# Modulation sums as products with a column of ones, and a third buffer for the modulation's weight rows

## The chip, the core and the metric

The kernel runs on one core of a Trainium2 chip. A core has five engines that work side by side, each in the order of its own queue: TensorE (PE in the profile, its weight loads PEld) multiplies, VectorE (DVE) and ScalarE (ACT) work element by element, GpSimd (POOL) does odd jobs, and SyncE (SP) issues the DMA transfers. SBUF is the working memory of 128 partitions; TensorE writes its results to PSUM, which is divided into banks. The metric is the time of one execution on the device in microseconds, as the median of several runs.

## What is computed

A decoder trunk of two layers on 256 tokens with 2048 channels, all in float32. In each layer six modulation vectors come from one condition vector `c`; they scale and shift the inputs of the two sub-layers and gate their outputs.

```python
cond = jax.nn.silu(c)
for l in range(DEPTH):
    mod = (jnp.einsum('bd,de->be', cond, w_ada[l]) + b_ada[l]).reshape(B, N_MOD, 1, D_MODEL)
    sh_m, sc_m, gt_m, sh_f, sc_f, gt_f = [mod[:, i] for i in range(N_MOD)]
    u = x * (1 + sc_m) + sh_m
    proj = u @ w_in[l]
    y_attn = sliding_window_attention(q, k, v, attn_sinks[l], cos, sin)
    y_rwkv, v_first = rwkv7_group(...)
    mix = jnp.concatenate([y_attn, y_rwkv], axis=-1) @ w_out[l]
    x = layer_norm(DEEPNORM_ALPHA * x + gt_m * mix, ln1_w[l], ln1_b[l])
    u = x * (1 + sc_f) + sh_f
    gate, up = jnp.split(u @ w_gate_up[l], 2, axis=-1)
    x = layer_norm(DEEPNORM_ALPHA * x + gt_f * ((jax.nn.silu(gate) * up) @ w_down[l]), ln2_w[l], ln2_b[l])
```

The modulation is a product of one vector of 2048 with a matrix of 2048 x 12288 in each layer, 201 MB of weights in all, each of which is used once.

## The kernel before

**The weight stream.** The large products (`w_in`, `w_out`, `w_gate_up`, `w_down`) read their weights tile by tile through `steps` (L364 on): a tile `raw` of 128 x 1024 comes in by DMA (L372, four buffers), ScalarE rounds it to `hi` (L380), VectorE takes the rest as `lo` (L381), and TensorE forms three products of 128 x 512 (L402, L403, L405) or, turned round, of 128 x 256 (L414 to L416).

**The modulation.** It isn't done by TensorE, as a product with one row would leave it nearly empty. A unit is half a modulation vector, 1024 columns (`ada_steps`). For each of 16 row blocks a tile `ast` of 128 x 1024 comes in (L253, 512 KB, two buffers), and VectorE adds `ast` times its piece of `cond`, one scalar for each partition, to the sum `aacc` (L255 for the first, L257 for the others). Then `ada_sums` adds up `aacc` over the partitions: each of the 8 blocks of 128 x 128 is transposed by TensorE into a PSUM bank (L277), ScalarE copies the transposed block onto itself with an accumulated sum over the row (L281, two instructions in the profile: the copy and the reading of the accumulator) into a column of `asum`, and VectorE adds the bias and stores the vector in `mods` (L284). There are 20 such units. The two first modulation vectors of layer 0 are needed before anything else and are made in the opening by `ada_first`, in five parts of 4, 4, 2, 4 and 2 column blocks with eight buffers of their own (L301, L306); each part calls `ada_sums` twice, and then `make_u` transposes the input (L354) and makes `u` of it (L358 to L361).

**Banks.** `bank()` gives out two PSUM banks in turn; in the opening one of the two is held for a projection, so that all calls of `bank()` share the other.

**Order.** The 20 units run beside the weight stream: the generator `ada_rest` is moved on by so many rows after each weight tile (`pump`), in the recurrence (`adv(AR)`), and after each step of the attention (`adv(AA)`). A note of dependence (`anchor`) places each L257 behind the last `lo` before it. Tile's planner simulates the whole program on a time line and from it gives each engine its fixed order; on the chip each engine then waits in that order. All transfers are issued by SP, in one order: a transfer whose buffer isn't free yet, or whose source isn't written, holds up what is behind it.

**The mixer and the attention.** A layer's mixer runs the recurrent group (decays, project, prepare, invert, recur, close) and the attention, in an order written out by hand (`ORDER`). `invert` sends small matrices through DRAM: nb from nscr (L727), a loop on GpSimd, tinv from ttl (L738), tm from tinv (L741). The attention has for each of four key heads `rotate` (a), `weigh` (b) and `gather` (c). `rotate` loads `qk` (L888, L889, one buffer), multiplies it by the cosines into `ra` (L894) and by the sines into `rb` (L895), and combines both to `qr` in four instructions (L898, L899). `gather` transposes the weights of four heads (L964 to L966), copies each from PSUM into a `pts` (L969 on ScalarE for odd heads, L971 on VectorE for even ones, three buffers) and multiplies with the values (L977 to L981), heads 0 and 1 first, then 2 and 3. The attention's pool takes the place of the pool that the recurrent group needs before.

Of the kernel before, what the change touches and what calls it, by code (L numbers as in the profile page):

```python
# [10 lines left out]
F32 = mybir.dt.float32  # L11
F32R = mybir.dt.float32r
I32 = mybir.dt.int32
AF = mybir.ActivationFunctionType
ALU = mybir.AluOpType
AX = mybir.AxisListType
# [3 lines left out]
P = 128  # L20
# [24 lines left out]
PARTS = (4, 4, 2, 4, 2)  # L45
LAG = 2
WB = (4, 3, 2)
RED = 1
AR = (3, 7)
AA = (1, 45)  # L50
AP = (0.65, 0.3)
# [16 lines left out]
def hybrid_trunk_kernel(  # L68
# [21 lines left out]
    def bank(name="mb", tag="mb"):  # L90

        if tag == "cb":
            return ps.tile([P, 512], F32, tag="cb", name=name)
        t = f"m{turn[0]}"
        turn[0] ^= turn[1]
        return ps.tile([P, 512], F32, tag=t, name=name, bufs=1)
# [149 lines left out]
    def ada_steps(l, mod, c0):  # L246

        src = w_ada[l].rearrange("(j p) n -> p j n", p=P)
        n0 = mod * D + c0
        acc = adap.tile([P, 1024], F32, tag="aacc", name="aacc")  # L250
        for j in range(KT):
            t = adap.tile([P, 1024], F32, tag="ast", name="ast", bufs=2)
            dma(t, src[:, j, n0:n0 + 1024])  # L253
            if j == 0:
                V.tensor_scalar_mul(acc, t, cond[:, 0:1])  # L255
            else:
                ins = V.scalar_tensor_tensor(acc, t, cond[:, j:j + 1], acc, ALU.mult, ALU.add)  # L257
                if anchor:
                    tc.add_manual_dep(ins.ins, anchor[0], order, reason="behind the weight stream")
            yield  # L260
        for _ in range(LAG):
            yield

        ada_sums(l, mod, c0, [acc[:, i * P:(i + 1) * P] for i in range(8)])
        done.add((l, mod, c0 // 1024))
        yield

    def ada_sums(l, mod, c0, blocks):

        col = mod * KT + c0 // P  # L270
        n = len(blocks)
        sm = adap.tile([P, 8], F32, tag="asum", name="asum", bufs=2)
        for q in range(0, n, 4):
            b = bank()
            m = min(4, n - q)
            for i in range(m):
                PE.transpose(b[:, i * P:(i + 1) * P], blocks[q + i], ident)  # L277
            for i in range(m):
                bi = b[:, i * P:(i + 1) * P]
                if RED:  # L280
                    S.activation(bi, bi, AF.Copy, accum_out=sm[:, q + i:q + i + 1])  # L281
            if not RED:
                V.reduce_sum(sm[:, q:q + m], b[:, 0:m * P].rearrange("p (i k) -> p i k", k=P), axis=AX.X)
        V.scalar_tensor_tensor(mods[l][:, col:col + n], sm[:, 0:n], 1.0 if mod in (1, 4) else 0.0,  # L284
                               prm(l, "b_ada", col, n), ALU.add, ALU.add)
        if mod in (2, 5):
            row = adap.tile([8, P], F32, tag="arow", name="arow", bufs=2)[0:n]
            rb = bank()
            PE.transpose(rb[0:n, 0:P], mods[l][:, col:col + n], ident)
            S.copy(row, rb[0:n, 0:P])  # L290
            dma(gates[l, mod // 3, c0 // P:c0 // P + n], row)
# [198 lines left out]
    def mixer(l, us, mixp, feeds):  # L490
# [33 lines left out]
        if l > 0:  # L524
# [3 lines left out]
            b = bank()  # L528
# [355 lines left out]
        def rotate(kv):  # L884
            qk = pt.tile([P, 2, 320], F32, tag="qk", name="qk", bufs=1)
            vt = pt.tile([P, 2, 64], F32, tag="vt", name="vt", bufs=4)
            qd = qkv[l].rearrange("t p n -> p t n")
            dma(qk[:, :, 0:256], qd[:, :, kv * 256:(kv + 1) * 256])  # L888
            dma(qk[:, :, 256:320], qd[:, :, AW + kv * 64:AW + (kv + 1) * 64])  # L889
            dma(vt, qd[:, :, AW + KVW + kv * 64:AW + KVW + (kv + 1) * 64])  # L890
            ra = pt.tile([P, 2, 10, 32], F32, tag="ra", name="ra", bufs=1)
            rb = pt.tile([P, 2, 10, 32], F32, tag="rb", name="rb", bufs=1)
            sv = qk.rearrange("p t (h d) -> p t h d", d=32)
            V.tensor_mul(ra, sv, cosk.unsqueeze(2).to_broadcast([P, 2, 10, 32]))  # L894
            V.tensor_mul(rb, sv, sink_.unsqueeze(2).to_broadcast([P, 2, 10, 32]))  # L895
            qr = pt.tile([P, 2, 6, 64], F32, tag="qr", name="qr", bufs=1)
            for t in range(2):
                V.tensor_sub(qr[:, t, 0:5, 0:32], ra[:, t, 0::2, :], rb[:, t, 1::2, :])  # L898
                V.tensor_add(qr[:, t, 0:5, 32:64], ra[:, t, 1::2, :], rb[:, t, 0::2, :])  # L899
            G.tensor_copy(qr[:, :, 5, :], qr[:, :, 4, :])  # L900
            qT = pt.tile([P, 3, T], F32, tag="qT", name="qT", bufs=2)
            for j0, nj in ((0, 2), (2, 1)):
                b = abank(0)
                for j in range(nj):
                    for t in range(2):
                        PE.transpose(b[:, j * T + t * P:j * T + (t + 1) * P],
                                     qr[:, t, 2 * (j0 + j):2 * (j0 + j) + 2, :].rearrange("p h d -> p (h d)"), ident)
                if j0 == 0:
                    S.copy(qT[:, 0:2, :].rearrange("p a t -> p (a t)"), b)
                else:  # L910
                    S.activation(qT[:, 2, :], b[:, 0:T], AF.Copy, scale=0.125)
            at[kv] = qT, vt
# [46 lines left out]
        def gather(kv):  # L959
            pp, vt = at[kv]  # L960
            pts = {}
            for h in range(4):
                b = abank(2)
                PE.transpose(b[:, 0:P], pp[1, h][:, 0:P], ident)  # L964
                PE.transpose(b[:, P:2 * P], pp[1, h][:, P:2 * P], ident)
                PE.transpose(b[:, 2 * P:3 * P], pp[0, h], ident)  # L966
                pts[h] = pt.tile([P, 3 * P], F32, tag="pts", name="pts", bufs=3)
                if h % 2:
                    S.copy(pts[h], b[:, 0:3 * P])  # L969
                else:  # L970
                    V.tensor_copy(pts[h], b[:, 0:3 * P])  # L971
            yb = abank(3)
            for h2 in range(0, 4, 2):
                o = (h2 // 2) * T
                two = [(h, slice(64 * (h % 2), 64 * (h % 2) + 64)) for h in (h2, h2 + 1)]
                for h, hs in two:
                    PE.matmul(yb[hs, o:o + P], lhsT=vt[:, 0, :], rhs=pts[h][:, 2 * P:3 * P], start=True, stop=True)  # L977
                for h, hs in two:
                    PE.matmul(yb[hs, o + P:o + 2 * P], lhsT=vt[:, 0, :], rhs=pts[h][:, 0:P], start=True, stop=False)
                for h, hs in two:  # L980
                    PE.matmul(yb[hs, o + P:o + 2 * P], lhsT=vt[:, 1, :], rhs=pts[h][:, P:2 * P], start=False, stop=True)  # L981
            for j in range(2):
                keep_y(2 * kv + j, yb[:, j * T:(j + 1) * T])
# [364 lines left out]
```

## Time and profile before

| | |
|---|---|
| median of 3 runs | 2715.88 us (2715.45 to 2717.28) |
| the profiled execution | 2716.41 us, its span 2714.6 us |
| first row tile of a unit issued | 56.4 us |
| last row tile of a unit issued | 1666.9 us |
| last modulation vector stored | 1754.3 us |
| row tiles of the 20 units, 512 KB each | 320 |
| blocks summed by L277, L281 | 192 |

The tables of the profile are read like this. A row of a stretch has its window, its length, and then for each engine the busy time with the count of instructions, the granted clock of TensorE, the busy share of the 16 DMA engines and their rate in GB/s. A row of a group has line, engine, operation, output and inputs, shape and count, then the busy time in us, the mean of one in ns, and the idle time of that engine just before, with what ended it. A row of the waits has who waited for whom: total in us, times, longest. A row in the order of time has the start and the length in us; instructions that follow one another with the same line are one row with their count; what stands in brackets is the engine's idle time ahead of it and what ended it. Matmul ends are modelled: a plain pass of 128 columns is shown with some 0.27 us, though the next may start 0.11 us after it.

### The profile page before, as it was taken

How to read it: one execution, taken by the hardware profiler on the slowest of the kernel's cores; microseconds unless marked ns; L12 is line 12 of the kernel's file. 1: busy time of each engine (PE TensorE's matmuls, PEld its weight loads, DVE VectorE, ACT ScalarE, POOL GpSimd, SP SyncE). 2: the span in 40 equal slices, each digit the busy share in tenths (PEclk: the TensorE clock that was granted, in tenths of full speed). 3: DMA queues.
4: the chain of work that ended last, by engine and by line, in shares of the span. 5: the costliest groups of instructions: out<-in, count | busy, mean ns of one | idle time of the engine just before them, and what ended most of it. 6: DMA issues, size and time to landing. Idle time of an engine off the chain costs nothing. (4 is left out here: it accounts for less than half of the span.)

```text
span 2714.6 us, 41774 instructions
## 1 busy us (share of the span) xinstructions
PE 2517.3 (93%) x15325; PEld 2103.9 (78%) x15325; DVE 1853.5 (68%) x2437; ACT 1188.4 (44%) x2029; POOL 180.0 (7%) x387
## 2 busy tenths in 40 slices
PE   3789998797999999999999989989899999999998
PEld 2787886575788888888889877867788888888887
DVE  6877767879777777777788677565764545545456
ACT  2364452434444444444445544534444444344442
POOL 1002111003000000000000022110120000000000
PEclk9799997798999999999999999979999999999999
DMA  9968667597888888889888586423746655566654
GB/s 310 382 193 254 203 197 225 179 331 250 313 318 308 303 307 304 294 302 309 304 287 288 175 251 204 116 75 130 258 163 190 190 190 190 194 191 189 190 190 148
DMA packets 351999, 637.49 MB, mean 235 GB/s; under 512 B 75894, under 2 KB 142898, under 8 KB 350258
## 3 DMA queue, kind: packets, MB, share of 16 engines
q1 hardware_dynamic: 351794, 634.82, 71.1%
q8 instruction: 120, 1.97, 0.3%
q14 instruction: 85, 0.70, 0.1%
HBM read 622.08 MB, written 12.62 MB: 234 GB/s over the span
## 5 line engine op out<-in xcount | busy, mean ns | idle before, releaser
L380 ACT CAST hi<-raw 128x1024 fp32r<-128x1024 f32 (+2 forms) x728 | 757.8, 1044 | 1097.6 <-PE acc L405 810.6
L381 DVE TENSOR_TENSOR lo<-raw,hi 128x1024 fp32r<-128x1024 f32 (+2 forms) x728 | 885.9, 1220 | 515.8 <-PE acc L403 335.2
L403 PE MATMUL acc<-lo,u 128*128 128x512 f32 x1568 | 515.7, 396 | 16.9 <-DVE lo L381 16.6
L405 PE MATMUL acc<-hi,u 128*128 128x512 f32 x1568 | 507.3, 392 | 0.0
L257 DVE SCALAR_TENSOR_TENSOR aacc<-ast,cond,aacc 128x1024 f32<-128x1024 f32 x300 | 388.7, 1296 | 136.2 <-DMA ast<-in_w_ada_dram 135.1
L402 PE MATMUL acc<-hi,u 128*128 128x512 f32 x1568 | 459.7, 395 | 2.4 <-ACT u L360 1.1
L403 PEld LDWEIGHTS acc<-lo,u 128*128 128x128 f32 x1568 | 294.6, 189 | 83.9 <-DVE lo L381 23.7
L402 PEld LDWEIGHTS acc<-hi,u 128*128 128x128 f32 x1568 | 295.8, 189 | 65.4 <-ACT u L360 1.8
L405 PEld LDWEIGHTS acc<-hi,u 128*128 128x128 f32 x1568 | 296.4, 189 | 62.3 <-issue 0.7
L403 PE MATMUL acc<-lo,ht 128*128 128x512 f32 (+1 forms) x720 | 243.7, 377 | 2.7 <-DVE lo L381 2.6
L405 PE MATMUL acc<-hi,ht 128*128 128x512 f32 (+1 forms) x720 | 242.3, 375 | 0.0
L414 PE MATMUL acc<-u,hi 128*128 128x256 f32 x720 | 206.4, 293 | 12.9 <-ACT hi L380 12.9
L402 PE MATMUL acc<-hi,ht 128*128 128x512 f32 (+1 forms) x720 | 217.1, 376 | 0.0
L415 PE MATMUL acc<-u,hi 128*128 128x256 f32 x720 | 205.6, 292 | 0.0
L416 PE MATMUL acc<-u,lo 128*128 128x256 f32 x720 | 193.7, 295 | 5.3 <-DVE lo L381 5.3
L403 PEld LDWEIGHTS acc<-lo,ht 128*128 128x128 f32 x720 | 135.1, 188 | 28.8 <-DVE lo L381 5.2
L414 PEld LDWEIGHTS acc<-u,hi 128*128 128x128 f32 x720 | 142.8, 199 | 16.7 <-ACT hi L380 13.6
L405 PEld LDWEIGHTS acc<-hi,ht 128*128 128x128 f32 x720 | 135.6, 188 | 24.3
L402 PEld LDWEIGHTS acc<-hi,ht 128*128 128x128 f32 x720 | 134.8, 188 | 24.3
L415 PEld LDWEIGHTS acc<-u,hi 128*128 128x128 f32 x720 | 142.6, 198 | 3.5 <-issue 2.6
L416 PEld LDWEIGHTS acc<-u,lo 128*128 128x128 f32 x720 | 134.4, 198 | 9.5 <-DVE lo L381 6.9
L1067 POOL TENSOR_TENSOR brs<-brs,mhalf 128x1 f32<-128x1 f32 x8 | 5.2, 655 | 1637.3 <-DVE brs L1066 851.5
(349 smaller groups left out, 2950.9 us busy)
## 6 DMA issues: line engine op xcount, KB each, us to landing
ast<-in_w_ada_dram SPq DMA_DIRECT2D x368, 512.0 KB
raw<-in_w_gate_up_dram SPq DMA_DIRECT2D x704, 256.0 KB
raw<-in_w_down_dram SPq DMA_DIRECT2D x176, 512.0 KB
raw<-in_w_in_dram SPq DMA_DIRECT2D x82, 512.0 KB
raw<-in_w_out_dram SPq DMA_DIRECT2D x64, 512.0 KB
raw<-in_w_in_dram SPq DMA_DIRECT2D x120, 256.0 KB
ast<-in_w_ada_dram SPq DMA_DIRECT2D x32, 256.0 KB
lnw<-in_ln_w_dram SPq DMA_DIRECT2D x4, 1024.0 KB
```

The costliest lines, as they stand in the source:

```text
L257: ins = V.scalar_tensor_tensor(acc, t, cond[:, j:j + 1], acc, ALU.mult, ALU.add)
L380: S.copy(h, fl)
L381: ins = V.tensor_tensor(r, fl, h.bitcast(F32), ALU.subtract)
L402: PE.matmul(bt, lhsT=xh, rhs=hi[:, c0:c0 + w], start=st, stop=False)
L403: PE.matmul(bt, lhsT=xh, rhs=lo[:, c0:c0 + w], start=False, stop=False)
L405: PE.matmul(banks[t][q][:, 0:w], lhsT=xl, rhs=hi[:, c0:c0 + w], start=False, stop=sp_)
L414: PE.matmul(bt, lhsT=hi[:, c0:c0 + w], rhs=xh, start=st and opens, stop=False)
L415: PE.matmul(bt, lhsT=hi[:, c0:c0 + w], rhs=xl, start=False, stop=False)
L416: PE.matmul(bt, lhsT=lo[:, c0:c0 + w], rhs=xh, start=False, stop=sp_ and closes)
L1067: G.tensor_tensor(rs[:, 0:1], rs[:, 0:1], mhalf[:, 0:1], ALU.pow)
```

## The change

`ada_sums` no longer transposes and adds up. It multiplies each block, as stationary operand, with the column `ones`, which is there already; the result is the sum over the partitions, one column of a PSUM bank for each block, and L284 reads the bank directly. `asum` and the other form of the sum (`RED`) go. `ast` gets a third buffer of 4 KB in each partition. To make room, `rotate` writes the product with the sines over `qk` itself, so that `rb` goes (2.5 KB), and `pts` has two buffers instead of three (1.5 KB).

```diff
-RED = 1
...
-            t = adap.tile([P, 1024], F32, tag="ast", name="ast", bufs=2)
+            t = adap.tile([P, 1024], F32, tag="ast", name="ast", bufs=3)
...
-        sm = adap.tile([P, 8], F32, tag="asum", name="asum", bufs=2)
-        for q in range(0, n, 4):
-            b = bank()
-            m = min(4, n - q)
-            for i in range(m):
-                PE.transpose(b[:, i * P:(i + 1) * P], blocks[q + i], ident)
-            for i in range(m):
-                bi = b[:, i * P:(i + 1) * P]
-                if RED:
-                    S.activation(bi, bi, AF.Copy, accum_out=sm[:, q + i:q + i + 1])
-            if not RED:
-                V.reduce_sum(sm[:, q:q + m], b[:, 0:m * P].rearrange("p (i k) -> p i k", k=P), axis=AX.X)
+        sm = bank()
+        for i in range(n):
+            PE.matmul(sm[:, i:i + 1], lhsT=blocks[i], rhs=ones, start=True, stop=True)
...
-            rb = pt.tile([P, 2, 10, 32], F32, tag="rb", name="rb", bufs=1)
             sv = qk.rearrange("p t (h d) -> p t h d", d=32)
             V.tensor_mul(ra, sv, cosk.unsqueeze(2).to_broadcast([P, 2, 10, 32]))
+            rb = sv
             V.tensor_mul(rb, sv, sink_.unsqueeze(2).to_broadcast([P, 2, 10, 32]))
...
-                pts[h] = pt.tile([P, 3 * P], F32, tag="pts", name="pts", bufs=3)
+                pts[h] = pt.tile([P, 3 * P], F32, tag="pts", name="pts", bufs=2)
```

## The prediction, made before the changed kernel was run

> **What bounds the kernel now.** I read the page first, then stretches of the span with the busy time of each engine, then the groups of the two lines that the change replaces, then the waits, and last single places in the order of time. All rows are of the profiled execution: 2716.4 us, of which the span is 2714.6 us; the median of the runs is 2715.88 us, 0.5 us lower.
>
> ```profile
> span 2714.6 us, 41774 instructions
> PE 2517.3 (93%) x15325; PEld 2103.9 (78%) x15325; DVE 1853.5 (68%) x2437; ACT 1188.4 (44%) x2029; POOL 180.0 (7%) x387
> ...
> core 0: us, PE busy (x) PEld busy (x) DVE busy (x) ACT busy (x) POOL busy (x), PEclk, DMA share, GB/s
> 60.00:130.00 70.00, 47.76 (x313) 45.34 (x312) 56.52 (x72) 23.69 (x51) 0.00 (x0) 0.80 1.06 381
> 690.00:1360.00 670.00, 666.76 (x3007) 548.61 (x3007) 498.22 (x466) 299.04 (x446) 0.00 (x0) 1.00 0.89 308
> 433.00:545.00 112.00, 84.92 (x742) 65.00 (x743) 92.81 (x226) 44.74 (x162) 14.80 (x36) 0.73 0.65 188
> 1360.00:1760.00 400.00, 377.63 (x3183) 332.27 (x3182) 290.34 (x430) 198.59 (x389) 48.02 (x108) 0.97 0.70 221
> 1760.00:2715.00 955.00, 918.97 (x4794) 756.32 (x4790) 532.93 (x716) 394.08 (x530) 38.12 (x56) 0.97 0.55 177
> ...
> 1754.32 0.17 DVE L284 SCALAR_TENSOR_TENSOR mods<-asum,par 128x8 f32<-128x8 f32 x1 [0.67 <-ACT mb L281]
> ```
>
> There is not one bound. The opening is bound by DMA (a share of 1.06). From 690 to 1360 us TensorE is busy for 666.76 of 670 us: what it is given more to do there lengthens the kernel. From 433 to 545 (layer 0's attention) VectorE leads with 92.81 of 112 us while TensorE waits. The modulation ends at 1754 us, so of the change only the attention pool touches the rest.
>
> **TensorE's price of the sums.** Groups and single rows of the lines concerned:
>
> ```profile
> L277 PE MATMUL mb<-ident,aacc 128*128 128x128 f32 x192 | 31.4, 300 | 21.3 <-DVE aacc L257 10.7 <-ACT mb L281 5.8 <-DVE aacc L306 4.8
> L710 PE MATMUL kb<-de,bkc 128*128 128x128 f32 x96 | 13.3, 284 | 0.0
> L281 ACT ACTIVATE mb<-mb 128x128 f32<-128x128 f32 x192 | 50.3, 262 | 44.1 <-PE mb L277 37.4 <-issue 3.4 <-DVE lo L381 0.4
> L281 ACT ACTIVATION_READ_ACCUMULATOR mb<-mb 128x1 f32 x192 | 36.6, 191 | 0.1
> ...
> 690.00:1360.00 670.00, 26.90 (x160) 1.00 0.89 308
> ...
> 832.74 1.02 PEld L277 LDWEIGHTS mb<-ident,aacc 128*128 128x128 f32 x8
> 1708.30 1.42 PEld L710 LDWEIGHTS kb<-de,bkc 128*128 128x128 f32 x12
> 1758.40 0.89 PEld L647 LDWEIGHTS ssb<-bones,kkn 128*64 128x64 f32 x14
> ```
>
> The 192 transposes are one pass each: 20 units of 8 blocks and 32 blocks in the opening. L710's loops issue 2 x 4 x 2 x 3 = 48 plain f32 products, and the row counts 96, so a plain f32 product takes two passes, each with its weight load. The price of a pass: L710's 12 loads of 128 columns lie (1.42 - 0.19)/11 = 0.111 us apart; L647, with half the columns of weights and only two moving columns, (0.89 - 0.14)/13 = 0.058 us. Half the weights, half the pace: the load sets it, not the moving columns. The new product has 128 columns of weights and one moving column, so I take 2 x 0.111 = 0.222 us, against (1.02 - 0.19)/7 = 0.119 us for a transpose in the row and 0.111 if its one load sets it as well. I take **+0.11 us a block**. The bounds are 2 x 0.058 - 0.119 = 0 and, with four such passes, 4 x 0.111 - 0.119 = +0.33.
>
> The row of L281 alone has 160 instructions between 690 and 1360 us, two a block: 80 blocks, 10 units, all in the full stretch: 80 x 0.11 = **+8.8** us. The other 10 units lie in the mixers and between, where TensorE has gaps: half of that, **+4.4** (0 to 8.8).
>
> The Trainium skill, "FP8 and Floating Point Precision", TensorE Precision Notes, gives a true FP32 product four passes through the array. The 96 for 48 products speaks against it here. By that rule the two terms would be three times as large, about +40 instead of +13.2; it is a rival below.
>
> ScalarE loses 50.3 + 36.6 = 87 us of work. It is busy 44% of the span and most of this lies beside full TensorE: **-1** (-4 to 0).
>
> **The opening.** There one PSUM bank serves both sums and the transposes of u, one after the other:
>
> ```profile
> 135.29 0.60 PE L277 MATMUL mb<-ident,aacc 128*128 128x128 f32 x4
> 137.55 0.66 PE L277 MATMUL mb<-ident,aacc 128*128 128x128 f32 x4 [1.66 <-ACT mb L281]
> 137.61 1.54 DVE L306 SCALAR_TENSOR_TENSOR aacc<-ast,cond,aacc 128x512 f32<-128x512 f32 x2
> ...
> 139.92 1.11 PE L354 MATMUL mb<-ident,xt 128*128 128x128 f32 x4 [1.72 <-ACT mb L281]
> ```
>
> From 135.29 to 139.92 two sums take 4.6 us. With products each is 8 loads (0.9 us), a result in PSUM and one short VectorE instruction, with a wait for the L306 ahead of it (0.77 us each): about 1.5 us, so 3.0, a gain of 1.6. There are five such parts; the first three are covered by DMA, and after the last two TensorE sets the pace: **-3** (0 to -8). Against it: the third buffer lets one more row of 0.5 MB into the opening, at 381 GB/s **+1.4** (0 to 2).
>
> **What the third buffer can free.** VectorE's waits for weight rows (L257) by stretch, 433 to 545, 1360 to 1760, 545 to 690 and 690 to 1360 us, in this order:
>
> ```profile
> DVE aacc L257 <- DMA ast<-in_w_ada_dram: 15.8, 14, 2.5
> ...
> DVE aacc L257 <- DMA ast<-in_w_ada_dram: 30.4, 17, 9.2
> ...
> DVE aacc L257 <- DMA ast<-in_w_ada_dram: 5.7, 9, 1.4
> ...
> DVE aacc L257 <- DMA ast<-in_w_ada_dram: 62.4, 48, 2.7
> ```
>
> The 62.4 us are worth nothing: TensorE is full there. The longest of the others:
>
> ```profile
> 1590.65 0.34 SPq L253 DMA_DIRECT2D ast<-in_w_ada_dram  x1
> 1599.48 1.28 SPq L738 DMA_DIRECT2D tinv<-ttl  x2
> ...
> 1602.04 0.41 SPq L253 DMA_DIRECT2D ast<-in_w_ada_dram  x1
> ...
> 1604.55 1.04 ACT L380 CAST hi<-raw 128x1024 fp32r<-128x1024 f32 x1 [1.84 <-DMA raw<-in_w_in_dram]
> ...
> 1608.38 1.28 DVE L257 SCALAR_TENSOR_TENSOR aacc<-ast,cond,aacc 128x1024 f32<-128x1024 f32 x1 [9.17 <-DMA ast<-in_w_ada_dram]
> ...
> 1609.81 1.09 PE L277 MATMUL mb<-ident,aacc 128*128 128x128 f32 x4 [7.32 <-DVE aacc L257]
> ...
> 1612.18 0.41 PE L415 MATMUL acc<-u,hi 128*128 128x256 f32 x1
> ...
> 1619.10 0.28 PE L416 MATMUL acc<-u,lo 128*128 128x256 f32 x1
> ```
>
> One queue (SP) issues everything in order. It stands 9 us at the store of tinv, which waits for GpSimd; the last row of a unit is behind it, VectorE waits 9.17 us for the row, and TensorE, also in order, stands 7.32 us before that unit's transposes. With a third buffer this row's place was free one row earlier, ahead of the store. What is late next is the weight tile cast until 1605.6, also issued behind the store, so 3.1 of the 7.32 stay and 4.2 go; the slow passes after the stall (0.41 for 0.28 us, until 1616) add some 2: **-6.3**. Two more of the kind:
>
> ```profile
> 437.47 1.09 PE L277 MATMUL mb<-ident,aacc 128*128 128x128 f32 x4 [3.35 <-DVE aacc L257]
> ...
> 1670.93 1.28 DVE L257 SCALAR_TENSOR_TENSOR aacc<-ast,cond,aacc 128x1024 f32<-128x1024 f32 x1 [6.28 <-DMA ast<-in_w_ada_dram]
> ...
> 1673.41 0.80 PE L403 MATMUL acc<-lo,u 128*128 128x512 f32 x1 [4.17 <-DVE lo L381]
> ```
>
> Of 3.35 and 4.17 us I take **-2.5** and **-3**; the second is the lo of a weight tile, queued on VectorE behind the waiting L257. In the attention stretch 13 us of the waits remain beside the first stall, on the engine that bounds it; half, **-6.5**. Of the 5.7 us around layer 0's normalisation, **-2**. Together **-20.3**; bounds 0 (each wait gives way to another) and -30.
>
> **The attention pool.** qk is now held until the four short L898/L899 are done, not L895 alone:
>
> ```profile
> 1805.79 0.36 SPq L888 DMA_DIRECT2D qk<-qkv  x1
> ...
> 1804.94 0.82 DVE L895 TENSOR_TENSOR rb<-qk,sink__147 128x640 f32<-128x640 f32 x1
> ...
> 1806.99 0.32 DVE L899 TENSOR_TENSOR qr<-ra,rb 128x160 f32<-128x160 f32 x1
> ```
>
> The next load would start at 1807.3 instead of 1805.79, and SP holds what is queued behind. That is 1.5 us per load at most, six loads that have one before them; most are hidden, since the next rotation waits for other things. With two pts the third copy waits for the products on the first; the third and fourth copies then run side by side on VectorE and ScalarE. Both together **+1.5** (0 to 8).
>
> **Sum.** 8.8 + 4.4 - 1 - 3 + 1.4 - 20.3 + 1.5 = -8.2 us: 2716.4 - 8.2 = **2708.2 us**.
>
> **Rivals.** *Even*: half of the 20.3 us comes back as other waits on the same one queue, since a wait there is for GpSimd and DMA and not for the row's place. 2708.2 + 10 = 2718.2 us. For it speaks that the tile of weights at 1604.55 was late too. *TensorE's price decides* (slower): the rows stay behind the same small transfers, and the units in the mixers pay their full 8.8. Only 8 of 20.3 us are freed: 2708.2 + 12.3 + 4.4 = 2724.9 us. It decides, with the bound given below, as soon as less than about 12 us of the waits go; the full stretch, where the third buffer can do nothing, is sure to pay. This is also the case in which the third buffer does not do what it says. *Four passes*: another 0.22 us for each of 80 blocks and half as much for the mixers' 80, +26.6: 2734.8 us.
>
> **How the numbers follow.** A measurement of this kernel can tell about 0.2% from no change, 5.4 us: faster is under 2710.4, slower over 2721.3. Forecast 0.42, even 0.28, TensorE's price 0.27, four passes 0.03. So faster 0.42, same 0.28, slower 0.30. The forecast's own range is 2697 to 2710.4, with 27 instead of 20 us of waits gone at its low end. The range, with the bounds of the waits above and the slower rival inside: 2697 to 2729.
>
> **What would show it.** The sums: 384 passes on the new line, 0.11 apart, and from 690 to 1360 the same work some 8.8 us longer; at 0.06 apart the price is nothing, at 768 passes four times as large as thought. The waits of L257 for rows outside the full stretch should fall from over 50 us to below 20, and no idle of several us should stand ahead of the sums on TensorE. If they fall and the time doesn't, VectorE's next wait has taken their place. In layer 1's attention, loads of qk should start up to 1.5 us later. I would be wrong if the order of the whole program, which is planned anew, moves stalls that I counted as fixed.

## The result: 2742.71 us, slower by 0.95%, and the profile after

The changed kernel takes 2742.71 us (median of 5 runs, 2735.74 to 2747.87) against 2715.88 us before; the ratio is 1.0095, with a 95% interval of 1.0077 to 1.0113. The forecast was 2708.2 us and its range ended at 2729. The profiled execution took 2747.87 us, the longest of the five. The page of the changed kernel (line numbers are lower by 10 below `ada_sums`):

```profile
span 2746.1 us, 41793 instructions
PE 2545.9 (93%) x15517; PEld 2132.4 (78%) x15517; DVE 1852.0 (67%) x2437; ACT 1126.5 (41%) x1645; POOL 175.8 (6%) x387
```

TensorE has 192 more instructions and is shown busy for 28.6 us more, ScalarE has 384 fewer; the span is 31.5 us longer. Next the groups and the waits for weight rows (433 to 545 and 1360 to 1760 us), and one unit's sum in the full stretch:

```profile
L273 PE MATMUL mb<-ones,aacc 128*128 128x1 f32 x384 | 50.3, 255 | 9.7 <-DVE aacc L296 7.4 <-DVE mods L274 2.1 <-DVE aacc L256 0.2
L256 DVE SCALAR_TENSOR_TENSOR aacc<-ast,cond,aacc 128x1024 f32<-128x1024 f32 x300 | 387.4, 1291 | 21.3 <-DMA ast<-in_w_ada_dram 20.5
```

```profile
DVE aacc L256 <- DMA ast<-in_w_ada_dram: 2.4, 3, 1.0
DVE aacc L256 <- DMA ast<-in_w_ada_dram: 11.4, 10, 3.8
```

```profile
1141.73 1.98 PEld L273 LDWEIGHTS mb<-ones,aacc 128*128 128x128 f32 x16
```

Two things went as forecast. A block takes two passes (384 records for 192 blocks), and a unit 1.98 us where the transposes' row showed 1.02: 0.96 us more, so some 9.6 us in ten units where 8.8 were forecast. And the waits went: 2.4 us in the attention for 15.8, 11.4 in layer 1's mixer for 30.4. Only the time did not come with them.

Where it went is seen when the start of the same instruction is taken from both traces. The table has the time lost or won against before in each stretch between two such starts (us, one profiled execution each; the other kernels are told of below). The stretches end at these instructions of the kernel before: the first L687 (211.1 us), the sixth L752 (421.4), the first L459 on ScalarE (495.9), the first L1224 (723.1), the first L1275 (1425.1), the 17th L687 (1560.4), the 14th L752 (1772.7), the fifth L1144 (1910.4) and the fourth L1189 (2700.1). Two things limit the reading. A single execution can lie 9 us off the median of its kernel (that of the third buffer and pool edits took 2706.71 us, its median is 2716.01). And a stretch doesn't hold just the same work in every kernel: the changed kernel sums 16 blocks in the first heads and 24 in the stretch after them, the kernel before 8 and 32. So a few us in one field tell little.

| kernel | opening | mixer 0 | heads 0 | to 723 | full stretch | to 1560 | mixer 1 | heads 1 | rest |
|---|---|---|---|---|---|---|---|---|---|
| changed kernel | -5.3 | +9.7 | **+7.3** | -7.4 | +6.0 | -7.1 | **+22.5** | +2.4 | +3.3 |
| product sums alone | -5.8 | +5.9 | **+13.5** | -5.1 | +15.3 | -4.3 | +3.0 | -2.7 | +4.7 |
| third buffer and pool edits | -3.3 | -1.4 | -1.0 | +1.2 | -5.5 | -1.1 | +1.0 | -0.5 | +0.6 |
| product sums, note of order | -8.4 | +3.2 | +1.4 | -6.6 | +12.2 | -4.2 | +0.9 | -8.1 | +3.5 |
| changed, note in both layers | -9.3 | +4.9 | +0.7 | -5.5 | +5.0 | -6.4 | +0.7 | -6.1 | +1.4 |
| changed, note in layer 0 | -6.2 | +5.8 | +0.4 | -3.5 | +4.5 | -5.5 | -1.6 | -1.8 | +3.2 |
| changed, note in layer 1 | -6.0 | +6.3 | **+7.3** | -7.6 | +4.5 | -7.2 | **+24.3** | -3.2 | +2.3 |
| changed, ytr later | -7.5 | +5.8 | **+13.4** | -3.3 | +4.4 | -5.5 | +0.9 | -5.4 | +2.2 |
| changed, five rows a step | -6.2 | +7.7 | **+7.7** | -1.9 | +4.4 | -7.1 | +0.6 | +2.8 | +3.9 |
| before, chain put ahead | -0.6 | -1.1 | **+11.1** | -3.6 | +1.7 | +2.3 | +3.9 | -1.7 | +1.7 |
| before, store put ahead | -0.2 | -1.5 | -0.1 | -5.9 | +4.2 | +0.7 | -19.2 | +4.5 | +0.1 |
| product sums, turn given back | -5.4 | +7.9 | -3.8 | +1.6 | +10.8 | -5.5 | +7.1 | -4.6 | +4.4 |
| changed, GpSimd's queue | -3.1 | +0.5 | +5.4 | -12.0 | +5.0 | -5.6 | -0.0 | +2.6 | +3.4 |

Two stretches are followed here, the first heads of layer 0's attention and layer 1's mixer. Layer 0's mixer loses 9.7 us too, but every other kernel with product sums in its units loses 0.5 to 7.9 us there, those that end up as fast as the kernel before among them; its cause stays open.

**The first heads.** SP, then VectorE, then TensorE of the changed kernel, in the order of time:

```profile
436.24 1.35 SPq L717 DMA_DIRECT2D nb<-nscr  x2
450.85 1.27 SPq L728 DMA_DIRECT2D tinv<-ttl  x2
453.70 1.27 SPq L731 DMA_DIRECT2D tm<-tinv  x2
455.06 1.05 SPq L252 DMA_DIRECT2D ast<-in_w_ada_dram  x2
456.20 0.38 SPq L878 DMA_DIRECT2D qk<-qkv  x1
```

```profile
443.95 0.42 DVE L710 TENSOR_TENSOR bv<-bnb,vx 128x256 f32<-128x256 f32 x1
457.44 0.71 DVE L735 STREAM_TRANSPOSE ytr<-tm 128x512 f32<-128x512 f32 x1 [13.07 <-DMA tm<-tinv]
...
462.82 0.82 DVE L883 TENSOR_TENSOR ra<-qk,cosk 128x640 f32<-128x640 f32 x1
```

```profile
465.15 1.16 PE L896 MATMUL acc<-ident,qr 128*128 128x128 f32 x3 [9.89 <-DVE qr L889]
```

The store of tinv of the last group waits until GpSimd's loop ends (at 450.83 us by the trace), and SP with it, from 437.6 to 450.85 us. Behind it stand the load of tm, two rows and only then the first head's `qk`, at 456.20. VectorE waits 13.07 us for tm with the rows and the rotation behind it, and TensorE 9.89 us for the rotated head. In the kernel before, SP issued these in the other order:

```profile
430.93 0.60 SPq L727 DMA_DIRECT2D nb<-nscr  x1
...
442.58 0.38 SPq L888 DMA_DIRECT2D qk<-qkv  x1
...
450.34 1.28 SPq L738 DMA_DIRECT2D tinv<-ttl  x2
```

Nothing in the diff names tinv or the loads of qk. The plan made anew for the whole program turned them. The same rows are turned in layer 1.

**Layer 1's mixer.** SP and TensorE of the changed kernel:

```profile
1630.82 12.49 SPq L252 DMA_DIRECT2D ast<-in_w_ada_dram  x7
...
1656.90 1.31 SPq L717 DMA_DIRECT2D nb<-nscr  x2
1658.26 1.17 SPq L362 DMA_DIRECT2D raw<-in_w_in_dram  x2
1670.73 1.28 SPq L728 DMA_DIRECT2D tinv<-ttl  x2
```

```profile
1632.18 1.97 PE L746 MATMUL m<-tm,yx 64*64 64x64 f32 x32 [5.88 <-DVE yx L742]
...
1652.87 1.19 PE L774 MATMUL mr<-bkt,ah 64*128 64x128 f32 x4 [5.01 <-DVE uv L770]
```

Seven rows come in one go and no weight tile for 27 us. VectorE adds the rows (1.29 us each) between the short steps of the recurrence, and TensorE waits for those steps.

### The profile page after: what moved, and what is told of

The parts are those of the page before. It is cut to its first block, busy times and chain, and to the rows that moved or that the text cites. A ratio compares the mean times of both kernels' runs of the same rounds, so it can differ in the third digit from the quotient of the medians.

```text
span 2746.1 us, 41793 instructions
## 1 busy us (share of the span) xinstructions
PE 2545.9 (93%) x15517; PEld 2132.4 (78%) x15517; DVE 1852.0 (67%) x2437; ACT 1126.5 (41%) x1645; POOL 175.8 (6%) x387
## 4 chain that ended last, share of the span: by engine, by line
PE 78%; DMA 9%; DVE 8%; ACT 2%; issue 2%; POOL 1%; SPq 1%; DVEq 0%; ACTq 0%; POOLq 0%
PE acc L393 20%; PE acc L395 20%; PE acc L392 19%; DMA ast<-in_w_ada_dram 3%; PE acc L406 3%; PE acc L404 3%; PE acc L405 3%; DMA raw<-in_w_in_dram 2%; DVE lo L371 2%; DVE aacc L256 1%; PE mb L273 1%; DMA raw<-in_w_out_dram 1%; DMA raw<-in_w_gate_up_dram 1%; PE mb L1211 1%; PE aa L674 1%
## 5 line engine op out<-in xcount | busy, mean ns | idle before, releaser
L393 PE MATMUL acc<-lo,u 128*128 128x512 f32 x1568 | 516.4, 395 | 10.8 <-DVE lo L371 10.7
```

What stands on the lines that cost most here:

```text
L393: PE.matmul(bt, lhsT=xh, rhs=lo[:, c0:c0 + w], start=False, stop=False)
```

## Experiments

The kernel before ran beside each of them, at 2714.3 to 2716.4 us. Ratios are to that, with their 95% intervals.

### The change taken apart

Four kernels, each the kernel before with a part of the change. **Product sums alone**:

```diff
-        sm = adap.tile([P, 8], F32, tag="asum", name="asum", bufs=2)
...
+        sm = bank()
+        for i in range(n):
+            PE.matmul(sm[:, i:i + 1], lhsT=blocks[i], rhs=ones, start=True, stop=True)
```

> The product sums alone, with two row buffers and the attention pool of before. Burst theory (the third buffer lets the plan pack rows into the latency-bound parts of the mixers, where VectorE is in order): only the price of the products (+6.4 us in the full stretch, as read from the changed kernel) and the gain in the opening (-5 us) are left, so 2710 to 2725 us, and no loss of tens of us between 1600 and 1800. Price theory (the products' two passes cost the time): nearly all of the +27 us is here, 2735 to 2745 us. Re-planning theory (any edit throws the stalls anew): anywhere within some 15 us of before, with losses and gains at other places than in the changed kernel.

Measured: 2743.63 us, 1.0113 (1.0096 to 1.0130). The whole loss is here, so the burst theory, which gave it to the third buffer, falls. The time lies where the price theory put it, but that theory doesn't explain it: the full stretch loses 15.3 us (9.6 of them passes), and 13.5 us are lost at the first heads, where TensorE stands:

```profile
461.71 0.47 PE L897 MATMUL acc<-ident,qr 128*128 128x128 f32 x1 [14.96 <-DVE qr L890]
```

**The third buffer with the two edits of the attention pool**, sums by transposes:

```diff
-            t = adap.tile([P, 1024], F32, tag="ast", name="ast", bufs=2)
+            t = adap.tile([P, 1024], F32, tag="ast", name="ast", bufs=3)
...
+            rb = sv
...
-                pts[h] = pt.tile([P, 3 * P], F32, tag="pts", name="pts", bufs=3)
+                pts[h] = pt.tile([P, 3 * P], F32, tag="pts", name="pts", bufs=2)
```

> The third row buffer with the two edits of the attention pool, sums by transposes as before. Burst theory: the loss between 1600 and 1800 us is here too, +25 to +40 us there, 2730 to 2745 us in all. Price theory: no loss, the row waits go, 2700 to 2718 us. Re-planning theory: within some 15 us of before, with the losses at places of its own.

Measured: 2716.01 us, 1.0004 (0.9987 to 1.0021). Its group of the row additions:

```profile
L257 DVE SCALAR_TENSOR_TENSOR aacc<-ast,cond,aacc 128x1024 f32<-128x1024 f32 x300 | 387.5, 1292 | 23.6 <-DMA ast<-in_w_ada_dram 22.9
```

The waits fall from 136.2 to 23.6 us and the time stays. Where the row waits were priced highest, in layer 1's mixer, the trace shows what took their place, first on VectorE, then on TensorE:

```profile
1595.89 0.71 DVE L745 STREAM_TRANSPOSE ytr<-tm 128x512 f32<-128x512 f32 x1 [7.03 <-DMA tm<-tinv]
...
1657.08 0.71 DVE L745 STREAM_TRANSPOSE ytr<-tm 128x512 f32<-128x512 f32 x1 [8.43 <-DMA tm<-tinv]
```

```profile
1596.66 0.58 PE L749 MATMUL m<-ytr,am 64*64 64x64 f32 x6 [6.64 <-DVE ytr L745]
...
1658.73 1.22 PE L599 MATMUL ab<-xwa,w2a 64*128 64x256 f32 x2 [7.65 <-DVE bv L720]
```

VectorE's waits for rows between 1360 and 1760 us fall from 30.4 to 6.2 us, but it now waits for tm, which comes behind the store of tinv (bv of the last line stands behind ytr on VectorE). TensorE is idle for 14.8 us in this mixer, against 12.4 us in the kernel before (1549.2 to 1762.6 and 1560.4 to 1772.7 us).

**The pool edits alone** (the last three lines of that diff):

> The two edits of the attention pool alone (the sine product over qk, two pts). Burst theory and price theory: within 5 us of before, 2713 to 2721 us. Pool theory (qk held longer delays the loads of the next head and what is queued behind them): +10 us or more, in the attentions at 430 to 545 and 1760 to 1830 us. Re-planning theory: within some 15 us, also at places that the edits don't touch.

Measured: 2717.19 us, 1.0009 (0.9992 to 1.0026): nothing that can be told from none; the prediction had +1.5.

**The changed kernel with two row buffers**:

> The changed kernel with two row buffers: product sums and the pool edits, without the third buffer. Burst theory: 2710 to 2725 us, no loss of tens of us between 1600 and 1800. Price theory and pool theory: as slow as the changed kernel, 2735 to 2748 us. Re-planning theory: the sum of the single edits doesn't add up.

Measured: 2743.22 us, 1.0109 (1.0092 to 1.0125), as slow as the changed kernel. In all kernels with product sums so far tinv stands ahead of the first head's loads in both layers, in the three with transposes behind them. That gave the next theory.

### The order of SP's queue

**Product sums alone, with one note of order.** The note only says which of the two SP issues first:

```diff
+                ins = dma(diagonal(tz, 2, q), tt[64 * q:64 * q + 64])
+                if g == 3:
+                    tc.add_manual_dep(ins.ins, first[0], order, reason="behind the first head's loads")
...
+            ins = dma(qk[:, :, 256:320], qd[:, :, AW + kv * 64:AW + (kv + 1) * 64])
+            if kv == 0:
+                first[:] = [ins.ins.name]
```

> The product sums alone, with one note of order added: SP issues the last group's store of tinv, which waits for GpSimd, only after the first head's loads of qk, as it did before the change. Queue theory (the sums by products made the plan issue that store ahead of the loads in both layers, and the first head waits for GpSimd): the 15 us stall of TensorE ahead of the first head's transposes in layer 0 falls below 5 us and the time falls by 10 to 15 us from the product sums alone, to 2728 to 2734 us; what is left over before is the two passes' price, some 9 us in the full stretch. Price theory (nothing but TensorE's passes): within 5 us of the product sums alone, 2739 to 2748 us.

Measured: 2717.24 us, 1.0004 (0.9990 to 1.0018): 26 us gone, about twice what was expected. By the traces 12.1 of them are at the first heads (+13.5 to +1.4), 5.4 at layer 1's heads, the rest in small parts.

**The changed kernel with the same note**:

> The changed kernel with the same note of order. Queue theory: 2727 to 2733 us, 10 to 15 us below the changed kernel. Price theory: within 5 us of the changed kernel, 2738 to 2748 us. Burst theory (third buffer's rows crowd VectorE in layer 1's mixer): some of the loss between 1600 and 1700 us stays whatever the order of the loads of qk, so above 2733 us.

Measured: 2708.91 us, 0.9981 (0.9964 to 0.9999): 33.8 us below the changed kernel, where 10 to 15 were expected, and 0.7 us from the forecast. SP and VectorE:

```profile
427.19 1.42 SPq L718 DMA_DIRECT2D nb<-nscr  x2
433.98 1.66 SPq L252 DMA_DIRECT2D ast<-in_w_ada_dram  x2
435.68 0.43 SPq L881 DMA_DIRECT2D qk<-qkv  x1
...
445.80 1.28 SPq L729 DMA_DIRECT2D tinv<-ttl  x2
```

```profile
442.73 0.86 DVE L888 TENSOR_TENSOR ra<-qk,cosk 128x640 f32<-128x640 f32 x1
...
460.47 0.71 DVE L738 STREAM_TRANSPOSE ytr<-tm 128x512 f32<-128x512 f32 x1
```

The loads go 8.5 us after nb, not 20; the rotation is done 15 us ahead of ytr, which then waits for nothing. The burst in layer 1's mixer went too, though the note doesn't name its rows: after a change in layer 0 all that follows is planned anew.

**Product sums in the opening only** (`ada_first` calls the new form, the units the old one):

> Product sums in the opening only (32 blocks); the 20 units are summed by transposes as before, two row buffers. Queue theory and price theory: the opening's gain of some 6 us and nothing else, 2708 to 2712 us, since neither the passes in the full stretch nor the order of SP's queue in the attention change. If the new plan as a whole costs the time, whatever edit brings it: 2720 us or more.

Measured: 2713.97 us, 0.9990 (0.9971 to 1.0009). The trace shows 5.5 us won in the opening; the change in time can't be told from none, and 2708 to 2712 us were expected.

**Product sums in the units only**:

> Product sums in the 20 units only, the opening by transposes as before, two row buffers. Queue theory: tinv's store stands ahead of the first head's loads again, so the whole loss without the opening's gain: 2745 to 2752 us. Price theory: the same, but with the loss in the full stretch and no stall of 10 us or more in layer 0's attention. If the loss came from the opening: near before, 2713 to 2720 us.

Measured: 2731.59 us, 1.0068 (1.0046 to 1.0089), 13 to 20 us below what was expected. The hold is there (10.2 us at the first heads), and the full stretch loses 9.5 us, but not 15.3; why this plan lost less there stays open.

### One layer at a time, and two surprises

**The note in layer 0 only, and in layer 1 only**, in the changed kernel:

```diff
-                if g == 3:
+                if g == 3 and l == 0:
```

> The changed kernel with the note of order in layer 0 only; in layer 1 the store of tinv still stands ahead of the first head's loads. Queue theory: layer 0's attention gains 12 us; layer 1's wait stays, about 6 us: 2712 to 2720 us, if the rows crowded into layer 1's mixer go with the new plan as they did with both notes; 2726 to 2734 us if they stay. If only both together matter: as slow as the changed kernel.

> The changed kernel with the note of order in layer 1 only; layer 0 as in the changed kernel, with seven row loads in one go in layer 1's mixer. Queue theory: only layer 1's attention gains, 4 to 7 us: 2735 to 2739 us; TensorE's stalls between 1620 and 1680 us (some 20 us against before) stay. If the crowded rows cost nothing: 2725 us or less.

Measured: layer 0 only 2712.26 us, 0.9985 (0.9975 to 0.9994); layer 1 only 2740.51 us, 1.0094 (1.0077 to 1.0111). The first lies at the low end of what was expected, the second 1.5 us above. With the note in layer 1 alone the seven rows and their +24.3 us are there again; with the note in layer 0 they are gone.

**The opening's products, the third buffer and the note together**:

> What the runs so far point to: product sums in the opening only, the 20 units by transposes as before, the third row buffer with the pool edits, and the note of order in both layers. Queue theory with the measured price of the passes (9 us in the full stretch): the changed kernel with both notes was at 2709 us, less 9 us for the passes not paid, so 2698 to 2706 us. If the passes' price is hidden (ScalarE's copies cost as much where it matters): 2706 to 2712 us.

Measured: 2706.17 us, 0.9959 (0.9945 to 0.9974), just above the 2698 to 2706 us of the queue theory. The full stretch gave what the passes cost (5.5 us won, where the changed kernel with the note lost 5.0), but layer 1's heads gave most of it back (+3.5 against -6.1).

**Before, with tinv's store put ahead of the first head's loads in layer 0**:

```diff
+            ins = dma(qk[:, :, 0:256], qd[:, :, kv * 256:(kv + 1) * 256])
+            if l == 0 and kv == 0:
+                tc.add_manual_dep(ins.ins, first[0], order, reason="behind the store of tinv")
...
             elif op[0] == "X":
+                if l == 0:
+                    head(3, st[3], nscr[3])
```

> The kernel before, transposes and all, with the cause added in layer 0 alone: the loads of the first head are held behind the last group's store of tinv (GpSimd's loop of that group moved ahead in the program so that it can be). Queue theory: a stall of 10 us or more ahead of the first head's transposes and 8 to 15 us more in all, 2724 to 2731 us. Price theory: nothing, within 5 us of before.

Measured: 2702.04 us, 0.9947 (0.9932 to 0.9962): faster by 14 us. A miss, and its trace says why it wasn't the test that was meant:

```profile
440.98 0.89 SPq L902 DMA_DIRECT2D vt<-qkv  x2
441.91 1.21 SPq L884 DMA_DIRECT2D qkv<-stg  x2
443.22 1.31 SPq L739 DMA_DIRECT2D tinv<-ttl  x2
444.58 0.61 SPq L896 DMA_DIRECT2D qk<-qkv  x1
```

GpSimd was done when SP came to the store, neither tm nor rows stood between, and qk went at 444.58 instead of 442.58. The first heads lose nothing (-0.1 us): the order on the queue costs nothing as long as what is waited for is there. What was won shows in layer 1, without any edit near it: the mixer is 19.2 us shorter between the same instructions and the heads behind it 4.5 us longer, 14.7 us together. TensorE's stalls of 7.32 and 4.17 us at 1602 and 1669, which the prediction had priced, aren't there (the longest in the mixer is 2.52 us). But that isn't the gain: over mixer and heads together TensorE is idle for 27.4 us before and 28.1 us here, as other waits took their place, while its busy time is 322.6 and 307.2 us, at a granted clock of 0.92 and 0.95. Why this plan's passes are shorter stays open.

### What holds the first head, and what the rows cost

**The changed kernel, with VectorE's ytr of the last group behind the first rotation** in layer 0, and SP left alone:

```diff
+                ins = V.transpose(yt.rearrange("p e s -> p (e s)"), tm.rearrange("p e s -> p (e s)"))
+                if g == 3 and l == 0 and level == 0:
+                    tc.add_manual_dep(ins.ins, first[0], order, reason="behind the first head's rotation")
```

> The changed kernel with one note on VectorE alone, in layer 0: the last group's ytr, which waits for tm, comes after the first head's rotation; SP still issues the store of tinv and the load of tm ahead of the loads of qk. If VectorE's place is what costs (13 us of waiting for tm with rows and rotation behind it): 2712 to 2722 us. If SP's order costs: the loads of qk are as late as in the changed kernel, 2730 us or more.

Measured: 2724.22 us, 1.0036 (1.0022 to 1.0050), between the two. SP and VectorE:

```profile
445.99 1.27 SPq L729 DMA_DIRECT2D tinv<-ttl  x2
448.84 1.27 SPq L732 DMA_DIRECT2D tm<-tinv  x2
450.21 1.04 SPq L252 DMA_DIRECT2D ast<-in_w_ada_dram  x2
451.35 0.38 SPq L881 DMA_DIRECT2D qk<-qkv  x1
```

```profile
454.26 1.28 DVE L256 SCALAR_TENSOR_TENSOR aacc<-ast,cond,aacc 128x1024 f32<-128x1024 f32 x1 [13.75 <-DMA ast<-in_w_ada_dram]
```

ytr is out of the way, and VectorE now waits 13.75 us for a row behind the same store: the first heads still lose 13.4 us. What holds them is SP's queue, not VectorE's place. The 18.5 us that went are by the trace those of layer 1's mixer (+0.9 for +22.5), where the seven rows are gone with the new plan.

**The kernel before, with the whole chain put ahead**: group 2's recurrence and group 3's inversion earlier in the hand-written order, the first loads of qk behind tm's load, the first rotation behind ytr:

```diff
-X Q2 a0 a1 b0 C2 a2 b1 c0 E2 a3 c1 I3
+X Q2 C2 I3 a0 a1 b0 a2 b1 c0 E2 a3 c1
```

> The kernel before, with the whole chain put ahead of the first head in layer 0: recurrence of group 2 and inversion of group 3 come earlier in the hand-written order, the first loads of qk stand behind the load of tm on SP, and the first rotation behind ytr on VectorE. Chain theory: a wait of 10 us or more of VectorE for tm ahead of the rotation, TensorE stands as long, and the time rises by 8 to 20 us, 2724 to 2736 us. If the place of the chain doesn't matter: within 5 us of before, or faster as the kernel with tinv's store alone put ahead was.

Measured: 2721.55 us, 1.0024 (1.0009 to 1.0040): slower by 6.5 us, 2.5 us short of what was expected. SP and TensorE:

```profile
453.42 1.28 SPq L742 DMA_DIRECT2D tm<-tinv  x2
...
455.42 0.43 SPq L892 DMA_DIRECT2D qk<-qkv  x1
...
459.44 1.98 PE L753 MATMUL m<-ytr,am 64*64 64x64 f32 x32 [9.41 <-DVE ytr L747]
```

With the old sums the first heads lose 11.1 us (this execution is the slowest of ten), so the hold doesn't need the product sums. Counting this one, eight of the kernels here have loads of the first head behind a store of tinv at which SP stands, and their first heads lose 7.3 to 13.8 us (two of them aren't in the table: the changed kernel with two row buffers, 13.8, and the products in the units only, 10.2). In the others in which SP issues these transfers the stretch is between 5.2 us shorter and 1.4 us longer.

**The changed kernel with five rows moved on at a step of layer 1's recurrences instead of seven** (`AR = (3, 5)`); layer 0 is planned as in the changed kernel:

> The changed kernel, in layer 1's recurrences five rows moved on at a step instead of seven, so that the seven rows in one go in layer 1's mixer are gone; layer 0's order is that of the changed kernel, with its stall. If the crowded rows cost what the trace suggests (20 us between 1560 and 1680): 2720 to 2728 us. If they are only where the loss shows: 2738 us or more.

Measured: 2728.47 us, 1.0044 (1.0027 to 1.0060), 0.5 us above what was expected: 14.2 us gone, by the trace in layer 1's mixer (+0.6 for +22.5), while the first heads still lose 7.7. Stretches of the mixer, first of the changed kernel, then of this one, where the last three columns are the granted clock, the DMA share and the rate:

```profile
1622.00:1682.00 60.00, 41.91 (x466) 35.57 (x465) 34.82 (x52) 13.83 (x32) 9.41 (x34) 0.72 0.52 158
1564.00:1798.50 234.50, 212.42 (x1986) 180.20 (x1986) 146.71 (x220) 94.32 (x170) 38.77 (x101) 0.91 0.57 174
```

```profile
1622.00:1682.00 60.00, 54.73 (x666) 48.12 (x665) 39.46 (x64) 26.59 (x54) 11.11 (x34) 0.94 0.61 181
1565.00:1778.00 213.00, 202.95 (x1988) 172.83 (x1988) 146.19 (x220) 94.13 (x170) 40.34 (x101) 0.97 0.63 192
```

The same work (1986 and 1988 products) takes 234.5 us with the seven rows in one go and 213.0 without. Of the 21.5 us between them 12 are idle time of TensorE (22.1 against 10.1 us), and 9.5 are products that are shown longer (212.42 against 202.95 us): in the 60 us around the burst the granted clock is lower as well, 0.72 against 0.94. The Trainium skill, "TensorE: Matmul & The Clock Gate", The HAM clock gate (the "warmup" mystery), says that the throttled state is the default and that activity releases it; by that rule a stall costs more than its length, and these rows agree.

**Product sums alone, where each unit gives back the turn of the two banks**, no note:

```diff
+        turn[0] ^= turn[1]
```

> The product sums alone, where each unit gives back the turn of the two PSUM banks (as the two transposed batches did before), and no note: with this the first head's loads stand ahead of tinv's store in layer 0, but not in layer 1. Chain theory: close to the product sums with the note, 2715 to 2725 us, against 2743.6 us for the product sums alone, though not one instruction is more or less. Price theory: 2739 us or more.

Measured: 2722.68 us, 1.0030 (1.0018 to 1.0043), 21 us below the product sums alone, with the same count of instructions on each of the engines. Only which of the two banks a tile gets changes, and with it the plan. SP in layer 0:

```profile
439.18 0.38 SPq L880 DMA_DIRECT2D qk<-qkv  x1
...
452.20 0.60 SPq L730 DMA_DIRECT2D tinv<-ttl  x1
```

The first head's loads stand ahead of the store again, and the first heads lose nothing (-3.8 us, where the product sums alone lose 13.5).

**tinv's store and tm's load issued by GpSimd**, no note, in the changed kernel and in the kernel with products in the opening only:

```diff
+                G.dma_start(diagonal(tz, 2, q), tt[64 * q:64 * q + 64])
...
+                G.dma_start(tm[BH[i]], tz[8 * i:8 * i + 8, 0:CH].rearrange("e s t -> s e t"))
```

> The changed kernel, with the stores of tinv and the loads of tm issued by GpSimd, after its own loop, instead of SP; no note of order. Queue theory: nothing on SP waits for GpSimd's loop any more, the loads of qk go when their buffer is free, the stall ahead of the first head's transposes in layer 0 is below 5 us and the time is that of the changed kernel with the note, 2705 to 2716 us, plus what GpSimd's issue costs at eight inversions (0 to 2 us each, not seen so far). If the hold on SP isn't the cause: 2730 us or more.

> Product sums in the opening only, transposes for the units, third row buffer and pool edits, no note of order, the stores of tinv and the loads of tm issued by GpSimd. Queue theory: as fast as the same kernel with the note, 2700 to 2710 us, or some us less, since no transfer on SP waits for GpSimd's loop in any of the eight inversions. If GpSimd's issue is slow: 2712 us or more.

Measured: 2714.86 us, 1.0004 (0.9992 to 1.0017), 27.9 us below the changed kernel; and 2695.32 us, 0.9915 (0.9884 to 0.9946), the fastest of all here, 19.0 us below the kernel before beside it (2714.33; four runs, 2680.59 to 2698.76). SP and TensorE of the first:

```profile
435.75 1.65 SPq L252 DMA_DIRECT2D ast<-in_w_ada_dram  x2
437.45 0.43 SPq L878 DMA_DIRECT2D qk<-qkv  x1
```

```profile
455.27 0.69 PE L896 MATMUL acc<-ident,qr 128*128 128x128 f32 x2 [6.90 <-POOL qr L890]
```

qk goes 7.6 us after nb (429.88 us) without any note. A new wait of 6.90 us is GpSimd's own: the copy of `qr` stands behind its transfers, and the first heads still lose 5.4 us (the second kernel gains 0.3 there). The Trainium skill, "DMA: Bandwidth & Descriptors", Issuing engines are not separate DMA queues, holds that starting transfers from several engines saves only the time that a sequencer takes to start one. By that rule the move should be worth next to nothing; here the load of qk no longer stood behind a transfer that waits for its data. How much of the 27.9 us that is the runs don't tell: by the traces most of it lies in layer 1's mixer (-0.0 for +22.5), where the seven rows are gone, as in other kernels that were planned anew.

## Why the prediction was wrong

**The passes: right.** Two a block, 0.96 us a unit in the full stretch. The rival of four passes falls with that price: a block pays for two weight loads. But the prediction's argument against it, 96 records for 48 products, doesn't hold. In the kernel before, records of plain float32 with 256 moving columns (L598, L599) start 0.216 us apart in the median, 0.84 ns a column, and those of the weight stream with 512 columns 0.23 us, 0.45 ns a column. So a plain record may well be two passes in one; with a single moving column that doesn't show.

**The pool: within the noise** (+2 us, which can't be told from none, for +1.5).

**The opening: right in sign.** The kernels with products there won 3.1 to 9.3 us in it by the trace, but two with transposes there 3.3 and 4.7 too; the kernel with products in the opening alone gained nothing that its runs can tell.

**The full stretch: half right.** The 62.4 us of row waits were called worth nothing, TensorE being full. The three traces with the third buffer and the old sums in the units all show it 5.5 us shorter than before; the seven with the third buffer and product sums lose 4.4 to 6.0 us. So the passes cost 10 to 11.5 us there and the waits were worth 5.5, and the changed kernel lost 6.0 us, not 8.8.

**The row waits: this step failed.** The prediction put it as "Together -20.3; bounds 0 (each wait gives way to another) and -30." Two things were wrong in it. The size: in the kernel with the third buffer and the old sums, 113 of 136 us of waits went and the time moved by no more than can be told (+0.8 us). The two mixer stalls priced at -6.3 and -3 became two of 6.64 and 7.65 us behind the waits for tm, and the mixer came out 1.0 us longer; the first heads, for which -2.5 and part of the -6.5 stood, came out 1.0 us shorter. The prediction's own bound, that each wait gives way to another, is what the trace shows in this mixer. And the end at 0: each stall was priced in the order of before, as if the rows around it stayed, and nothing worse than "another wait" was let in. In its place the runs showed two new stalls that the new order made: the hold of the first head behind tinv's store, and the seven rows in layer 1's mixer.

What each cost is known less well than the two together. The note in layer 0 takes both away, and 30.4 us (2742.71 to 2712.26). Five rows a step or ytr moved takes the burst away, and 14.2 or 18.5 us (2728.47, 2724.22); what is left between those and the note in layer 0, 16.2 or 12.0 us, goes to the hold. The note in layer 1 brings 2.2 to 3.4 us more; with it the whole way from the changed kernel to 2708.91, 33.8 us, is covered. But each of these kernels was planned anew elsewhere too, and by the traces of the first heads alone the hold costs the changed kernel 7 us (+7.3 against +0.4 with the note) and the one with ytr moved 13.

With the note the kernel came out 0.7 us from the forecast, but not by its terms. The product sums with the note cost 0.8 us against the kernel before (forecast 8.8 + 4.4 - 1 - 3 = 9.2), and third buffer and pool brought 8.3 us on top of them (2717.24 - 2708.91; forecast -20.3 + 1.4 + 1.5 = -17.4). The two terms were too large by about as much (8.4 and 9.1 us), so that the number was met is luck.

**The rivals.** "TensorE's price decides" had the sign and 2724.9 us, for another reason; the passes were paid, but the loss was the order. "Even" named what layer 1's mixer shows with the third buffer and the old sums, other waits on the same queue for GpSimd, but it had no loss. The sentence that it would be wrong if the plan made anew moved stalls that were counted as fixed was the one that came true, and it had no price and no chance.

**What stays open**: why the plan turned these transfers. That it hangs on little is shown by the turn of the banks alone. Open too is what layer 0's mixer loses, and the exact shares of the two stalls.

## What to carry to other kernels

Where a planner fixes one order for the whole program, price an edit with its re-planning as a case of its own, of either sign (here -14 to +34 us), and compare the order of the queues before and after ahead of any theory about the edit. A transfer that waits for a slow engine belongs on a queue on which nothing urgent stands behind it, or behind a note of order. A wait of an engine is worth its length only if something on the path waits for that engine; 113 us of row waits went here and the time stayed; in layer 1's mixer waits for tm took their place.

## What was not expected of the hardware

A product of 128 x 128 float32 weights with a single moving column takes two weight loads and goes at their pace: 16 loads in 1.98 us for eight products, 0.12 us a load, as in the row of the transposes with 128 moving columns (8 loads in 1.02 us). Stalls of TensorE can cost more than their length: in layer 1's mixer 12 us more of idle time came with 9.5 us more of busy time for the same work, and in 60 us of it the granted clock was 0.72 instead of 0.94.
